# Stores of weight halves leave SP's DMA queue for ACT's and POOL's

## The chip, the cores and the metric

The kernel runs on one core of a Trainium2 chip. The metric is the device time of one execution in microseconds. Five engines run beside each other and meet through semaphores: PE (matrix products), DVE and POOL (elementwise work, POOL cannot read the matrix accumulators), ACT (activations, copies, casts) and SP, which here does nothing but start DMA transfers. Each engine, SP too, works its own list of instructions strictly in order: an instruction that waits holds up all that stand behind it on that engine. A DMA transfer is started by an instruction on some engine's list, and from there on runs by itself on the core's 16 DMA engines.

## The reference

One decoder layer on 2048 tokens of width 1024, in float32:

```
proj = x @ w_in                                  # 3592 columns, split over three mixers
y    = [GatedDeltaNet(4 heads) | dilated window attention(4) | differential attention(4)] @ w_out
x    = LayerNorm(alpha * x + y)
u    = causal depthwise conv3(x @ w_up)          # 2 x 2752 columns, gate and value
f    = (silu(gate) * value) @ w_down
out  = LayerNorm(alpha * x + f)
```

The gated delta rule is computed in chunks with a triangular inverse per chunk and a state carried from chunk to chunk. The window attention merges three dilations by their log-sum-exp; the differential attention subtracts two softmax maps.

## The kernel before

**Tiling.** Tokens come in four blocks of 512 (`NB = 4`, `TB = 512`). Channels lie on the 128 partitions. A product of a 128-column weight tile with a token block sums over eight slices of 128 (`KD = 8`) and fills one accumulator bank of 128x512.

**Three matmuls for one.** To keep float32 accuracy each operand is split into a rounded head and a rest: `hi` is the float32r cast, `lo` the difference. Each slice costs three matmuls, `whi*xhi`, `whi*xlo`, `wlo*xhi` (lines 206 to 208; for the output projections 1158, 1159, 1161).

**Weights** (`Dense.weights`, lines 127 to 162). A weight tile is handled as two halves of 128x512. The first time it is needed, each half is loaded by SP (`wraw`, line 151), ACT casts it to the head `whi` (line 153) and POOL subtracts to get the rest `wlo` (line 154). From job `c` of the plan on (`dn.keep = True`, line 1300) heads and rests of a tile with a key are also stored to DRAM, to `whi_d` and `wlo_d` (line 161), so that the later token blocks load them ready-made (line 148) and need neither ACT nor POOL. A head or rest may be overwritten only when its matmuls are done and its store has landed.

**Buffers.** Up to the end of the delta-rule phase raw halves, heads and rests have rings of 6, 4 and 4 buffers (`NRAW`, `NHALF`). Then all three kinds share one ring of 14 (`NW = 14`, line 1328). A half takes three of them, so a load can be at most between four and five halves ahead of the buffers it takes over.

**Stages.** The first phase does input projections and the first attention blocks (`FIRST`, line 1374). The second (`SECOND`) runs the delta rule: inverses, chunk preparation and the recurrence, with the projections of later blocks woven in; job `A3` there is the first whose weights are stored. The third (`THIRD`, line 1376) has the remaining attention blocks `w1 d1 A2 d2 w2 w3 d3` and the feed-forward blocks `f0` to `f3`, one per 512 tokens. Block `f0` meets every `w_up` and `w_down` tile for the first time, so it loads raw weights, splits and stores them; `f1` to `f3` load the stored halves. The part of `f2` that projects the mixers' output of the last token block (`attend(3)`) needs the attention block `d3` finished.

**What sets the order.** The code is written as jobs, but the place of each instruction on its engine is chosen when the program is built, by a scheduler that plays the program through a timeline of its own and takes what it holds to be ready. Attention work is mixed with feed-forward products in this way. Each DMA started from SP or ACT is also given one of eight shared completion counters, each started from POOL one of another eight; an instruction that starts a transfer on a counter waits until the counter's last transfer has landed, unless that is known already.

Some lines are named later: line 736 loads keys for the differential attention, lines 833 and 818 are its scores and its values on PE, line 835 its exponentials on ACT, line 700 stores its queries and keys, and line 595 scales the delta rule's output on POOL.

Of the kernel before, what the change touches and what calls it, by code (L numbers as in the profile page):

```python
# [27 lines left out]
def cast(x):  # L28
    return x.bitcast(F32)
# [81 lines left out]
class Dense:  # L111
# [15 lines left out]
    def weights(self, src, k=KD, m=P, pool=None, key=None):  # L127


        nc = self.nc  # L130
        n = k // 2 * m
        shape = lambda w: w.rearrange("p (k m) -> p k m", k=k // 2)

        def put(dt, name):
            if pool:
                w = pool.tile([P, TB], dt, tag=name, name=name, bufs=12)
            elif self.ring:
                w = self.wp.tile([P, TB], dt, tag="w", name=name, bufs=self.ring)
            else:
                w = self.wp.tile([P, TB], dt, tag=name, name=name, bufs=NRAW if name == "wraw" else NHALF)  # L140
            return shape(w[:, 0:n])

        his, los = [], []
        for i in range(2):
            if key in self.kept:
                hi, lo = put(F32R, "whi"), put(F32R, "wlo")
                for part, d in zip((hi, lo), self.kept[key]):
                    nc.sync.dma_start(out=cast(part), in_=cast(shape(d[:, i * n : i * n + n])))
            else:
                raw = shape((self.wp.tile([P, TB], F32, tag="w" if self.ring else "wraw", name="wraw", bufs=self.ring or NRAW))[:, 0:n])  # L150
                nc.sync.dma_start(out=raw, in_=src[:, i * (k // 2) : (i + 1) * (k // 2)])
                hi, lo = put(F32R, "whi"), put(F32R, "wlo")
                nc.scalar.copy(hi, raw)  # L153
                nc.gpsimd.tensor_tensor(out=lo, in0=raw, in1=hi, op=ALU.subtract)  # L154
            his.append(hi)
            los.append(lo)
        if key is not None and self.keep and key not in self.kept:
            self.kept[key] = [self.tc.dram_tile([P, 1024], F32R, name=name) for name in ("whi_d", "wlo_d")]
            for parts, d in zip((his, los), self.kept[key]):
                for i in range(2):  # L160
                    nc.sync.dma_start(out=cast(shape(d[:, i * n : i * n + n])), in_=cast(parts[i]))
        return Halves(his), Halves(los)

    def split(self, raw, pool=None, tag="x", bufs=None):
# [1290 lines left out]
```

## Time and profile before

| what | value |
|---|---|
| runs | 3291.5 us median of 3 (3281.3 to 3293.2) |
| profiled execution, its own time | 3290.28 us |
| span of that execution | 3288.5 us |
| PE busy | 3033.3 us, 92% of the span |
| DVE, ACT, POOL busy | 1870.7, 1354.4, 660.0 us |
| DMA moved | 659.29 MB, 200 GB/s over the span |
| stores of heads and of rests | 170 and 170, 256 KB each, the first at 745.5 us, the last at 1881.0 us |

The profile's page gives the busy time of each engine, the chain of work that ended last, and groups of instructions. Further views of the trace are used below: a table by stretch (busy time of each engine, number of instructions, granted PE clock, share of the DMA engines' time, GB/s), the chain of waits for a stretch, and lists of who waited for whom, for how many us in total, how many times, and the longest. A busy PE is not a PE at its peak: matmuls overlap, so a group's mean duration is longer than its share of the engine's time.

### The profile page before, as it was taken

Reading aid. Unit: us, or ns where it says so; the run is one execution under the profiler, and the core shown is the slowest. Engines: PE = TensorE matmul, PEld = TensorE weight load, DVE = VectorE, ACT = ScalarE, POOL = GpSimd, SP = SyncE. Lnnn points to the kernel's source line nnn. Section 1 sums busy time; section 2 is a strip of 40 time slices with the busy share of each in tenths; the row PEclk is TensorE's granted clock in tenths of the full one; section 3 lists DMA queues with packets and bytes.
Section 4 is the critical chain, followed back from the end, with each engine's and each line's share of the span. In section 5 each row is a group of like instructions: output and inputs, shape, how many; then the busy total and the mean of one; then the engine's idle time right before and its main releaser. Section 6 shows DMA issues by size and latency. Waiting matters only on the chain.

```text
span 3288.5 us, 43511 instructions
## 1 busy us (share of the span) xinstructions
PE 3033.3 (92%) x14476; PEld 2318.8 (71%) x14476; DVE 1870.7 (57%) x3392; ACT 1354.4 (41%) x3188; POOL 660.0 (20%) x571
## 2 busy tenths in 40 slices
PE   7898989998597798898899899999999999999998
PEld 5676867786476675565656677778866668888887
DVE  2562759665346245656746675557884444474446
ACT  3653553644144134645744332235653432122213
POOL 4563545442230012242212200000000000000001
PEclk9999989999688898998999999999999999999999
DMA  6546364546797776666677676666874545776554
GB/s 207 168 141 213 121 211 138 156 138 209 247 306 249 240 242 201 199 205 209 203 226 235 215 251 198 183 183 195 261 220 154 162 142 189 243 240 194 192 186 147
DMA packets 474209, 659.29 MB, mean 200 GB/s; under 512 B 75169, under 2 KB 201633, under 8 KB 473217
## 3 DMA queue, kind: packets, MB, share of 16 engines
q1 hardware_dynamic: 473984, 656.52, 63.2%
q8 instruction: 115, 1.88, 0.2%
q14 instruction: 110, 0.89, 0.1%
HBM read 500.82 MB, written 155.39 MB: 200 GB/s over the span
## 4 chain that ended last, share of the span: by engine, by line
PE 56%; DMA 12%; ACT 4%; DVE 3%; issue 2%; SPq 2%; POOL 1%; ACTq 0%; POOLq 0%; DVEq 0%
PE d L208 9%; PE d L206 9%; PE d L207 9%; PE rp L1158 6%; PE rp L1159 6%; PE rp L1161 5%; DMA wraw<-in_w_up 5%; PE bank L818 3%; DMA wraw<-in_w_down 3%; PE bank L833 2%; ACT whi L153 2%; PE bank L997 1%; DMA ks<-fk_d 1%; PE bank L1004 1%; PE bank L767 1%
## 5 line engine op out<-in xcount | busy, mean ns | idle before, releaser
L206 PE MATMUL d<-xhi,whi 128*128 128x512 f32 x2144 | 865.6, 404 | 41.1 <-ACT whi L153 16.4
L208 PE MATMUL d<-xhi,wlo 128*128 128x512 f32 x2144 | 861.3, 402 | 27.8 <-DMA wlo<-wlo_d 14.4
L207 PE MATMUL d<-xlo,whi 128*128 128x512 f32 x2144 | 858.9, 401 | 1.1 <-DVE xlo L169 1.1
L154 POOL TENSOR_TENSOR wlo<-wraw,whi 128x512 fp32r<-128x512 f32 x370 | 504.1, 1367 | 1471.1 <-ACT whi L153 1331.5
L206 PEld LDWEIGHTS d<-xhi,whi 128*128 128x128 f32 x2144 | 412.9, 193 | 153.0 <-ACT whi L153 26.2
L208 PEld LDWEIGHTS d<-xhi,wlo 128*128 128x128 f32 x2144 | 412.0, 192 | 136.8 <-POOL wlo L154 23.3
L207 PEld LDWEIGHTS d<-xlo,whi 128*128 128x128 f32 x2144 | 412.7, 192 | 102.8 <-issue 17.8
L153 ACT CAST whi<-wraw 128x512 fp32r<-128x512 f32 x370 | 227.7, 618 | 390.8 <-DMA wraw<-in_w_up 118.5
L1159 PE MATMUL rp<-wlo,hhi 128*128 128x512 f32 x704 | 280.9, 400 | 2.0 <-POOL wlo L154 2.0
L1158 PE MATMUL rp<-whi,hhi 128*128 128x512 f32 x704 | 268.1, 402 | 12.9 <-ACT whi L153 11.9
L1161 PE MATMUL rp<-whi,hlo 128*128 128x512 f32 x672 | 263.7, 396 | 0.0
L776 ACT ACTIVATE bank<-bank,nm 128x512 f32<-128x512 f32 (+3 forms) x320 | 190.1, 594 | 100.9 <-DVE nm L772 65.2
L1090 ACT COPY ub<-d 128x512 f32<-128x512 f32 x172 | 100.8, 586 | 315.9 <-PE d L208 315.3
L772 DVE TENSOR_REDUCE nm<-bank 128x1 f32<-128x512 f32 (+3 forms) x288 | 164.7, 598 | 96.1 <-PE bank L767 89.6
L843 POOL TENSOR_SCALAR_AFFINE_SELECT pd<-pd 128x128 f32<-128x128 f32 x64 | 32.5, 512 | 854.9 <-DVE pd L839 851.1
L839 DVE SCALAR_TENSOR_TENSOR pd<-pe,f_nlam,pd 128x512 f32<-128x512 f32 (+3 forms) x160 | 124.0, 782 | 138.3 <-ACT pe L835 109.6
L1158 PEld LDWEIGHTS rp<-whi,hhi 128*128 128x128 f32 x704 | 131.7, 189 | 55.4 <-ACT whi L153 19.1
L1159 PEld LDWEIGHTS rp<-wlo,hhi 128*128 128x128 f32 x704 | 133.5, 190 | 39.2 <-issue 6.9
L365 DVE SCALAR_TENSOR_TENSOR yc<-ub,i_taps,yc 128x512 f32<-128x512 f32 x144 | 156.3, 1086 | 3.3
L1168 DVE TENSOR_TENSOR r<-r,rp 128x512 f32<-128x512 f32 x152 | 101.8, 684 | 91.5 <-PE rp L1161 87.0
L1161 PEld LDWEIGHTS rp<-whi,hlo 128*128 128x128 f32 x672 | 127.3, 189 | 31.2 <-issue 4.8
L818 PE MATMUL bank<-pd,fv 128*64 128x512 f32 (+3 forms) x320 | 143.4, 553 | 0.0
(281 smaller groups left out, 4545.7 us busy)
## 6 DMA issues: line engine op xcount, KB each, us to landing
whi<-whi_d SPq DMA_DIRECT2D x486, 256.0 KB
wlo<-wlo_d SPq DMA_DIRECT2D x486, 256.0 KB
whi_d<-whi SPq DMA_DIRECT2D x170, 256.0 KB
wlo_d<-wlo SPq DMA_DIRECT2D x170, 256.0 KB
wraw<-in_w_gdn SPq DMA_DIRECT2D x128, 256.0 KB
ks<-fk_d SPq DMA_DIRECT2D x160, 196.0 KB
wraw<-in_w_up SPq DMA_DIRECT2D x86, 256.0 KB
wraw<-in_w_down SPq DMA_DIRECT2D x50, 256.0 KB
```

The costliest lines, as they stand in the source:

```text
L153: nc.scalar.copy(hi, raw)
L154: nc.gpsimd.tensor_tensor(out=lo, in0=raw, in1=hi, op=ALU.subtract)
L206: nc.tensor.matmul(out=ps, lhsT=whi[:, k], rhs=xhi[k], start=(k == 0), stop=False)
L207: nc.tensor.matmul(out=ps, lhsT=whi[:, k], rhs=xlo[k], start=False, stop=False)
L208: nc.tensor.matmul(out=ps, lhsT=wlo[:, k], rhs=xhi[k], start=False, stop=(k == KD - 1))
L365: nc.vector.scalar_tensor_tensor(out=yc, in0=ub[:, j : j + TB], scalar=self.taps[:, mt, j : j + 1], in1=yc, op0=ALU.mult, op1=ALU.add)
L772: nc.vector.tensor_reduce(out=o, in_=s[:, 0:nf], axis=mybir.AxisListType.X, op=ALU.min)
L776: nc.scalar.activation(out=s[:, 0:n], in_=s[:, 0:n], func=AF.Exp, scale=-1.0, bias=o, accum_out=den[:, b, m, qt : qt + 1])
L818: nc.tensor.matmul(out=po[64 * hh : 64 * hh + 64, q0:], lhsT=v[:, 64 * hh : 64 * hh + 64], rhs=pd[hh][:, q0:], start=start, stop=stop)
L1158: nc.tensor.matmul(out=ps, lhsT=hi[:, sl], rhs=whi, start=first, stop=False)
L1159: nc.tensor.matmul(out=ps, lhsT=hi[:, sl], rhs=wlo, start=False, stop=last and lo is None)
L1161: nc.tensor.matmul(out=ps, lhsT=lo[:, sl], rhs=whi, start=False, stop=last)
```

## The change

In `Dense.weights` the four stores of a tile are started from other engines: those of the heads from ACT, those of the rests from POOL. Nothing that is computed, loaded or stored differs; the transfers have the same sizes and addresses.

```
-            for parts, d in zip((his, los), self.kept[key]):
+            for eng, parts, d in zip((nc.scalar, nc.gpsimd), (his, los), self.kept[key]):
                 for i in range(2):
-                    nc.sync.dma_start(out=cast(shape(d[:, i * n : i * n + n])), in_=cast(parts[i]))
+                    eng.dma_start(out=cast(shape(d[:, i * n : i * n + n])), in_=cast(parts[i]))
```

The scheduler then lays the whole program out anew from there. Three places follow.

The first is SP's list in `f0`, while raw halves of `w_down` are loaded between the attention's keys (`ks`) and values (`fv`). Before:

```order
L736 DMA ks<-fk_d 98x4x128
L151 DMA wraw<-in_w_down 128x512
L161 DMA whi_d<-whi 128x512
L161 DMA wlo_d<-wlo 128x512
L161 DMA whi_d<-whi 128x512
L151 DMA wraw<-in_w_down 128x512
L826 DMA fv<-fv_d 128x128
L161 DMA wlo_d<-wlo 128x512
L161 DMA whi_d<-whi 128x512
L151 DMA wraw<-in_w_down 128x512
```

And with the change:

```order
L736 DMA ks<-fk_d 98x4x128
L151 DMA wraw<-in_w_down 128x512 x2
L826 DMA fv<-fv_d 128x128
L151 DMA wraw<-in_w_down 128x512
L736 DMA ks<-fk_d 98x4x128
L869 DMA y_d<-ob 128x512
L151 DMA wraw<-in_w_down 128x512 x2
```

Between one load of a raw half and the next there stood a store of a head and mostly one of a rest; now the loads follow each other, two in a row at places.

The second is ACT's list in `f0`, among the exponentials of the attention (line 776) and the copies of the convolution (lines 1090, 1091). Now there stands, where before only the casts stood:

```order
L153 CAST whi<-wraw 128x512
L161 DMA whi_d<-whi 128x512
L776 ACTIVATE bank_9714,den<-bank_9714,nm 128x256
L153 CAST whi<-wraw 128x512
L161 DMA whi_d<-whi 128x512
L776 ACTIVATE bank_9713,den<-bank_9713,nm 128x128
L776 ACTIVATE bank_9715,den<-bank_9715,nm 128x384
L776 ACTIVATE bank_9712,den<-bank_9712,nm 128x512
L153 CAST whi<-wraw 128x512
L161 DMA whi_d<-whi 128x512
L1090 COPY ub<-d 128x512
```

Each store stands right behind its cast or one or two instructions later. POOL's list alternates the subtraction and the store of its result in the same way.

The third is PE's list in `f2`, at the end of the attention block `d3`. Before, its last scores (line 833) and values (line 818) stood among products of `f2`:

```order
L208 MATMUL d<-xhi,wlo 128x512
L206 MATMUL d<-xhi,whi 128x512
L833 MATMUL bank_9712<-qs,ks 128x128
L207 MATMUL d<-xlo,whi 128x512
L208 MATMUL d<-xhi,wlo 128x512
L206 MATMUL d<-xhi,whi 128x512
L207 MATMUL d<-xlo,whi 128x512
L818 MATMUL bank_9715<-pd,fv 64x256
```

With the change the products end earlier, and the attention's last 96 matmuls (61 of line 833, 33 of line 818, 2 of line 865) stand in one piece, of which this is the beginning:

```order
L208 MATMUL d<-xhi,wlo 128x512
L833 MATMUL bank_9713<-qs,ks 128x512
L818 MATMUL bank_9715<-pd,fv 64x128
L833 MATMUL bank_9712<-qs,ks 128x512
L818 MATMUL bank_9715<-pd,fv 64x512
L833 MATMUL bank_9713<-qs,ks 128x512
L833 MATMUL bank_9712<-qs,ks 128x512
```

Part of the attention that stood inside `f0` now stands in `f1` and `f2`: PE's list from the first product of `f0` to the first of `f1` has 2149 matmuls instead of 2352.

## The prediction

> **What bounds the kernel now.** I read first the page's shares of the chain of waits, then the table by stretch from the first store to the end, then the chain inside the stretch that the first told me to look at, and last the lists of waits. On the page the chain lies on PE for 56% and on DMA for 12%, and the line under it names the raw loads of `w_up`, which are used in one stretch only:
>
> ```profile
> PE 56%; DMA 12%; ACT 4%; DVE 3%; issue 2%; SPq 2%; POOL 1%; ACTq 0%; POOLq 0%; DVEq 0%
> ```
>
> The table's columns are the stretch, its length, busy time and number of instructions of PE, weight loads, DVE, ACT and POOL, the granted PE clock, the DMA engines' share and GB/s:
>
> ```profile
> 745.00:1200.00 455.00, 351.36 (x2178) 286.06 (x2177) 197.81 (x441) 148.33 (x366) 79.15 (x69) 0.85 0.80 254
> 1200.00:1300.00 100.00, 87.13 (x426) 63.83 (x424) 59.64 (x108) 40.30 (x97) 27.02 (x21) 0.91 0.65 203
> 1300.00:1420.00 120.00, 107.39 (x403) 69.91 (x403) 77.18 (x180) 77.08 (x207) 36.42 (x32) 0.99 0.64 200
> 1420.00:1500.00 80.00, 77.36 (x296) 50.10 (x296) 41.92 (x52) 35.14 (x76) 31.91 (x30) 1.00 0.62 201
> 1500.00:1640.00 140.00, 119.83 (x429) 83.96 (x427) 94.57 (x206) 96.96 (x265) 38.16 (x28) 0.90 0.67 207
> 1640.00:1764.00 124.00, 122.10 (x448) 75.10 (x448) 58.36 (x91) 60.94 (x120) 23.25 (x25) 1.00 0.74 228
> 1764.00:1880.00 116.00, 106.52 (x445) 73.15 (x445) 81.45 (x119) 50.79 (x105) 37.00 (x32) 0.97 0.68 215
> 1880.00:3288.00 1408.00, 1395.96 (x6380) 1080.97 (x6379) 824.50 (x1450) 477.50 (x1100) 22.01 (x27) 1.00 0.62 197
> ```
>
> Behind 1880, where no half is stored any more, PE idles for 12 of 1408 us. In `f0`, 1200 to 1880, it idles for 680 - 620.3 = 59.7 us, nearly all of it in four rows (12.9, 12.6, 20.2, 9.5), and in three of these the clock is below 1. The delta-rule stretch before idles for 104 us, at a clock of 0.85. Inside `f0` the chain and one of its turns read (start, us, what):
>
> ```profile
> by line: DMA wraw<-in_w_up 21.8%; DMA wraw<-in_w_down 12.5%; ACT whi L153 6.6%; PE bank L818 5.6%; PE rp L1158 5.0%; issue 4.9%; PE rp L1159 4.3%; PE rp L1161 4.1%; PE bank L833 3.3%; DMA ks<-fk_d 2.8%; SPq L161 2.7%; PE d L208 2.6%; PE d L
> ```
>
> ```profile
> 1546.89 3.88 DMA wraw<-in_w_down
> ...
> 1550.85 0.63 ACT whi L153
> ...
> 1551.49 0.32 SPq L161
> ...
> 1551.86 4.97 DMA wraw<-in_w_down
> ```
>
> This is the bound. A load lands, ACT casts it, SP, which has been waiting for that cast in order to store it, starts the store, and only then the next load, which stands behind the store in SP's list. One half is in flight at a time, 4.97 us from load to load here, although the ring would hold four. SP's waits between 1300 and 1900 say the same (us in total, times, longest):
>
> ```profile
> SPq L161 <- ACT whi L153: 185.7, 78, 4.5
> SPq L161 <- POOL wlo L154: 37.6, 65, 1.1
> ```
>
> **The change part by part.** *The chain in `f0`.* The stores go from SP's list and with them the 223 us that SP waits in them. A load then waits for buffers alone. Three of 14 buffers go to a half, so load n takes over one whose user was four or five halves ahead: the subtraction of half n-4, or a head or rest whose matmuls and store are done. Four loads can be in flight, and a turn of load, cast and subtraction counts once for four halves. PE and the other engines set the pace. How much idle time stays is shown by the rows of `f0` where the chain did not decide: 1.9 of 124 us (1.5%) and 2.6 of 80 us (3.3%). On 620 us of PE work that is 9 to 20 us. I take 18, because bare runs of products in the new order use up halves faster than the mean. Gain 59.7 - 18 = 42 us; bounds 0 (another chain as long) and 50.
>
> *The clock.* Busy time times the missing share of clock is 87.13 x 0.09 + 107.39 x 0.01 + 119.83 x 0.10 + 106.52 x 0.03 = 24 us in `f0`. The rows with least idle time have 1.00, so shorter gaps should give some of it back: I take half, 12 us, bounds 0 and 24.
>
> *Two lists that become longer.* The prices come from these rows (count, then minimum, median and maximum in ns):
>
> ```profile
> L161 SPq DMA_DIRECT2D whi_d<-whi x170: 319/320/3069, 745.5 to 1879.6; - x170
> L153 ACT CAST whi<-wraw x128: 601/620/650, 1200.6 to 1878.9; 128x512 fp32r<-128x512 f32 x128
> L154 POOL TENSOR_TENSOR wlo<-wraw,whi x128: 1263/1286/2255, 1201.3 to 1879.6; 128x512 fp32r<-128x512 f32 x128
> ```
>
> ACT gets 128 stores in `f0`. No store stands on ACT yet; from below I bound it by SP's minimum of 0.319 us, from above by SP's 3.07. At the median, the nearest row, it is 41 us, beside 361 busy of 680 (the rows' sum), so it is hidden: ACT's spare time covers up to 2.5 us a store. Queued behind are casts, exponentials and copies of the convolution, each 0.32 us later. POOL gets as many, of which no row shows the like. Lower bound again 0.319. Upper bound is POOL's longest operation of this size, 2.26; I take 1.3, about its usual one. `f0` without the idle time, and without the attention that the new order takes out of it (203 matmuls at 620.3 us for the rows' 2447, about 50 us), lasts some 575 us, 4.5 a half, which leaves 3.2 us beside the subtraction. So both bounds are hidden and the cost is nothing; above 3.2 us POOL would be the new bound. The Trainium skill, "DMA: Bandwidth & Descriptors", section "Latency and other measured facts", gives about 1 us to the first byte for DMAs issued from GpSimd and 0.6 us for the hardware path; no run so far shows the former, and with it the sum stays the same.
>
> *The delta-rule stretch.* Of the 42 stores outside `f0` nearly all lie in 745 to 1200. PE's waits there that a quicker weight path could shorten, and the one that a fuller POOL could lengthen:
>
> ```profile
> PE vp L656 <- POOL wlo L154: 17.4, 6, 8.9
> PE yp L598 <- POOL on L595: 16.5, 4, 6.9
> PE vp L655 <- ACT whi L153: 8.8, 2, 7.0
> PE d L206 <- ACT whi L153: 6.6, 1, 6.6
> ```
>
> The first, third and fourth are 33 us, an upper bound of the gain. Against it, 42 x (0.32 + 1.3) = 68 us of new work lie on engines that the recurrence waits for; were a third of it on the path, 23 us would be lost. DMA is 80% busy there, so transfers begun earlier partly wait for each other instead. I take 0, bounds -23 and 33.
>
> *The end of `d3`.* The new order has 61 scores and 33 values in one piece in `f2`, with no product between them:
>
> ```profile
> L833 PE MATMUL bank<-qs,ks x128: 221/396/505, 2396.4 to 2693.4; 98*128 98x512 f32 x104, 98*128 98x384 f32 x8, 98*128 98x256 f32 x8, 98*128 98x128 f32 x8
> L818 PE MATMUL bank<-pd,fv x128: 272/592/643, 2423.6 to 2701.0; 128*64 128x512 f32 x104, 128*64 128x384 f32 x8, 128*64 128x256 f32 x8, 128*64 128x128 f32 x8
> L835 ACT ACTIVATE pe<-bank x64: 273/597/603, 2418.7 to 2693.6; 128x512 f32<-128x512 f32 x52, 128x384 f32<-128x384 f32 x4, 128x256 f32<-128x256 f32 x4, 128x128 f32<-128x128 f32 x4
> ```
>
> PE needs 61 x 0.396 + 33 x 0.592 = 44 us, ACT 61 x 0.597 = 36. With three banks in turn PE stays the longer, and the loss is 0; if each score waited for the exponential before it, it would be 36. I take 6.
>
> The sum: 42 + 12 + 0 - 6 = 48 us off the profiled execution's 3290.3 gives **3242 us**. That execution is 1.2 us below the median of the runs, so nothing is added.
>
> **The rivals.** *Only issue time is saved.* The loads wait again, for buffers whose stores are still on the way, and what goes is SP's own step in the chain: 2.7% of 680 = 18 us, 3272 us. For it: a buffer is released only by a landed store, and POOL's stores are unmeasured. Against it: the ring is four halves deep, and behind 1880 the same ring serves products at 1% idle. The Trainium skill, "DMA: Bandwidth & Descriptors", section "Issuing engines are not separate DMA queues", says that starting DMAs from several engines saves only the sequencer's time to start them, usually small; it is the rule that speaks against this change, and by it the sum would be this rival's 18 us. The trace speaks against it: what SP loses are 223 us of waiting, with 128 x 0.32 = 41 us of issue per kind of store.
>
> *Slower: ACT waits for SP's transfers.* In the delta-rule stretch 34 of the 40 head stores of the projections in `A3` and `o0` wait on a counter last used by a transfer of SP's. Such transfers take long there:
>
> ```profile
> 755.69 4.47 DMA whi_d<-whi
> 811.48 11.33 DMA qk<-qk_d
> 878.65 13.78 DMA fk_d<-sy
> ```
>
> If each of the 34 holds ACT for 4.5 us, the shortest of these, ACT loses 153 us in a stretch where it has 307 spare, and casts, exponentials and state copies of the recurrence stand behind. With half of it on the path the loss is 76 us and the time 3290 - 48 + 76 = 3318. It decides from 2.8 us a store. Against it: a counter comes round after eight transfers, so mostly the earlier one has landed.
>
> *The displaced attention.* The end of `d3` costs 36 us in place of 6: 3272 us. For it speaks the bare piece, which nothing covers; against it, that three banks take the scores in turn, so that PE need not wait for the exponential just before.
>
> **How the numbers follow.** Forecast 66%, only issue time 14%, displaced attention 7%, ACT's waits 13%. About 0.5%, 16 us, can be told from no change here, so faster means below 3275. The forecast lies there with all of its weight, the two cases at 3272 with half: 66 + 10 = 76% faster. The other half and a quarter of ACT's waits are the same: 14%. Slower: 10%. The forecast's own range is 3205 to 3270: at the low end all 24 us of clock and a quarter of the delta-rule bound come in, at the high end half of the gain in `f0` fails. With the rivals at 3272 inside and half of the slower case outside, the range is 3198 to 3288.
>
> **What would show it.** Right: in a table of the changed kernel, `f0` ends some 90 to 110 us earlier (48 and the moved attention), its chain no longer names raw loads, SP waits for PE in its loads, PE's idle time from 1200 on is near 30 us in all. Wrong: stores on POOL above 3 us; ACT waiting for DMA in line 161; the delta-rule stretch ending more than 20 us later; a gap on PE in the bare piece of `d3`.

## The result and the profile after

The changed kernel takes **3213.5 us** (median of 4 runs, 3209.9 to 3217.7), the kernel before on the same chip 3292.3 us (median of 4, 3281.3 to 3293.2). The ratio is 0.977, with a 95% interval from 0.976 to 0.979: 2.3% faster. The time lies inside the range and 28.5 us below the forecast of 3242. The profiled execution of the changed kernel took 3217.7 us, the one of before 3290.3, so the two traces differ by 72.6 us, and these are what has to be found in them.

The page of the changed kernel, first the two queues of its DMA transfers that are new (packets, MB, share of 16 engines), then the chain of work that ended last by engine:

```profile
q10 hardware_dynamic: 24480, 44.58, 3.8%
q0 software_dynamic: 13600, 44.58, 3.7%
...
PE 62%; DMA 7%; DVE 5%; ACT 2%; issue 1%; SPq 1%; POOL 1%; ACTq 0%; DVEq 0%; POOLq 0%
```

The stores have queues of their own, 44.58 MB each. DMA in the chain went from 12% to 7%, PE from 56% to 62%.

The table by stretch of the changed kernel (columns as in the prediction). `f0` is now 1184.6 to 1714.6, from its first cast to the last store; in the kernel before these two were 1200.6 and 1881.0:

```profile
745.00:1184.60 439.60, 341.98 (x2119) 275.97 (x2119) 191.27 (x426) 142.02 (x355) 96.03 (x106) 0.85 0.80 256
1184.60:1300.00 115.40, 113.62 (x589) 89.14 (x588) 84.75 (x148) 60.40 (x143) 63.59 (x65) 1.00 0.82 267
1300.00:1420.00 120.00, 118.86 (x489) 87.25 (x488) 84.33 (x175) 77.95 (x200) 65.00 (x71) 1.00 0.76 252
1420.00:1560.00 140.00, 134.99 (x535) 94.81 (x534) 82.76 (x105) 70.02 (x154) 75.95 (x87) 0.98 0.73 238
1560.00:1714.60 154.60, 143.78 (x616) 114.34 (x615) 123.47 (x223) 95.43 (x246) 54.28 (x56) 0.97 0.79 260
1714.60:2690.00 975.40, 970.43 (x4484) 718.32 (x4483) 598.77 (x1157) 392.29 (x915) 10.42 (x27) 1.00 0.62 196
2690.00:2740.00 50.00, 48.39 (x123) 15.28 (x121) 26.25 (x37) 35.16 (x67) 2.68 (x6) 1.00 0.28 82
```

In `f0` PE is busy for 511.3 of 530 us, so it idles for 18.7 where it idled for 59.7. The transfers run at 238 to 267 GB/s there, where the rows of before showed 200 to 228.

The 72.5 us of span split into three pieces. From the first cast of `f0` to the end, before 2087.9 us and now 2031.4, PE's idle time fell from 72.2 to 37.4 us: 34.8. Its busy time fell from 2015.7 to 1994.0: 21.7. And `f0` begins at 1184.6 and not at 1200.6: 16.0.

The last piece is not all waiting that went. Ahead of the first cast of `f0` PE now runs 5609 matmuls and not 5660, the others stand behind it, and it is busy there for 1005.8 us instead of 1017.6; its idle time there fell from 183.0 to 178.8. Over the whole span PE's idle time fell by 39.0 us, and its busy time, for the same 14476 matmuls, by 33.5.

What SP waits for in `f0`, and the chain there, in the changed kernel:

```profile
SPq L736 <- PE bank L767: 92.3, 24, 8.5
SPq L826 <- PE bank L818: 52.9, 11, 7.4
SPq L151 <- POOL wlo L154: 37.1, 19, 4.5
SPq L151 <- PE d L208: 36.2, 13, 3.7
```

```profile
by line: PE d L206 9.4%; PE d L208 9.4%; PE d L207 9.2%; PE rp L1158 8.2%; PE rp L1159 8.1%; PE rp L1161 7.9%; PE bank L818 5.1%; DVE nm L772 3.7%; PE bank L767 3.5%; DMA wraw<-in_w_up 3.5%; DVE yv L1095 2.8%; PE bank L833 2.5%; ACT bank L7
```

Line 161 is gone from SP's list. SP now waits for buffers, of keys and values (lines 736, 826) and of raw halves (line 151), most of them held by PE's own work. The chain is PE's products; of the raw loads, which carried 34% of it, those of `w_up` are at 3.5% and those of `w_down` below 1%.

The price of the stores on their new engines (count, then minimum, median and maximum in ns, first and last start), from the answers on `whi_d` and `wlo_d`:

```profile
L161 ACTq DMA_DIRECT2D whi_d<-whi x170: 326/326/614, 742.4 to 1712.9; - x170
```

```profile
L161 POOL DMA_DIRECT2D wlo_d<-wlo x170: 542/559/855, 746.0 to 1714.6; - x170
```

### The profile page after: what moved, and what is told of

Read it like the earlier page. It is cut to its first block, busy times and chain, and to the rows that moved or that the text cites. A ratio compares the mean times of both kernels' runs of the same rounds, so it can differ in the third digit from the quotient of the medians.

```text
span 3216.0 us, 43559 instructions
## 1 busy us (share of the span) xinstructions
PE 2999.8 (93%) x14476; PEld 2310.5 (72%) x14476; DVE 1883.0 (59%) x3392; ACT 1358.5 (42%) x3188; POOL 751.0 (23%) x741
## 3 DMA queue, kind: packets, MB, share of 16 engines
q10 hardware_dynamic: 24480, 44.58, 3.8%
q0 software_dynamic: 13600, 44.58, 3.7%
## 4 chain that ended last, share of the span: by engine, by line
PE 62%; DMA 7%; DVE 5%; ACT 2%; issue 1%; SPq 1%; POOL 1%; ACTq 0%; DVEq 0%; POOLq 0%
PE d L206 10%; PE d L207 10%; PE d L208 10%; PE rp L1158 6%; PE rp L1159 6%; PE rp L1161 6%; PE bank L818 4%; PE bank L833 2%; PE bank L767 1%; PE bank L997 1%; DMA whi<-whi_d 1%; PE bank L1004 1%; PE bank L958 1%; DMA fq_d<-sy 1%; DVE nm L772 1%
## 5 line engine op out<-in xcount | busy, mean ns | idle before, releaser
L839 DVE SCALAR_TENSOR_TENSOR pd<-pe,f_nlam,pd 128x512 f32<-128x512 f32 (+3 forms) x160 | 113.5, 715 | 168.1 <-ACT pe L835 142.6
```

## The experiments

All kernels compute and store everything. Each is laid out anew by the scheduler, so each carries an order of its own; the table at the end shows how far these orders differ. Ratios are to runs of the kernel before on the same chip, with 95% intervals. Diffs of the first six are against the kernel before, the others against the changed kernel.

### Heads alone

The stores of the heads go to ACT, those of the rests stay on SP.

```
-            for parts, d in zip((his, los), self.kept[key]):
+            for eng, parts, d in zip((nc.scalar, nc.sync), (his, los), self.kept[key]):
```

> Heads are stored from ACT, rests stay on SP. Theory 1 (what counts is which store stands ahead of the next load in SP's list): in f0 the store that is left there is that of the rest of the half before last, so two loads can be in flight; a turn of load, cast and subtraction, 4.0 + 0.6 + 1.3 us, counts for two halves, 3.0 us each, which is less than the 4.1 us a half that f0 took with the whole change. Most of the gain: 3215 to 3235 us. Theory 2 (SP saves issue time, so gain goes by the number of stores moved): half the gain, near 3253 us.

Measured: 3219.1 us, ratio 0.9795 (0.9765 to 0.9825): nearly the whole gain. What SP waits for in its `f0`:

```profile
SPq L161 <- POOL wlo L154: 225.9, 109, 4.8
```

SP waits for 226 us in the rests' stores (230 of 532 us in all rows of line 161, where it was 328 of 680 before), and the kernel loses next to nothing by it. Its list tells why. Here it is in time (start, us):

```profile
1405.04 0.38 SPq L826 DMA_DIRECT2D fv<-fv_d  x1
1405.47 0.45 SPq L151 DMA_DIRECT2D wraw<-in_w_up  x1
1407.68 0.32 SPq L161 DMA_DIRECT2D wlo_d<-wlo  x1
1408.06 0.42 SPq L151 DMA_DIRECT2D wraw<-in_w_up  x1
```

The store at 1407.68 comes 2.2 us after the load ahead of it. A load takes about 4 us (3.88 in the prediction's turn), the cast 0.62, the subtraction 1.29, so that store is of an earlier half, whose rest was still on its way when this load began. Two loads are in flight; from load to load it is 2.6 us in these rows, where the turn quoted of before took 4.97.

### Rests alone

The mirror image: rests on POOL, heads on SP.

```
+            for eng, parts, d in zip((nc.sync, nc.gpsimd), (his, los), self.kept[key]):
```

> Rests are stored from POOL, heads stay on SP. Theory 1: the store of a head still stands between its load and the next one, one half in flight, 4.0 + 0.6 + 0.3 us and more a half in f0: 3275 to 3295 us, and SP waits about as long for casts in line 161 as before (some 220 us). Theory 2: half the gain, near 3253 us.

Measured: 3292.6 us, ratio 1.0018 (1.0006 to 1.0030): no gain at all. What SP waits for in its `f0`, and a piece of its list:

```profile
SPq L161 <- ACT whi L153: 245.1, 92, 4.9
```

```profile
1513.93 0.33 SPq L151 DMA_DIRECT2D wraw<-in_w_up  x1
1517.87 0.32 SPq L161 DMA_DIRECT2D whi_d<-whi  x1
1518.29 0.37 SPq L151 DMA_DIRECT2D wraw<-in_w_up  x1
```

Load, 4 us, store of the head, next load: one half in flight, as before. The two runs take the same number of stores, 170, off SP's list, so the time that SP spends on starting them is the same in both; one gains 2% and the other nothing. The gain is not issue time. SP's waiting is not the loss either: in all rows of line 161 it waits for 230 us of the 532 of `f0` in the one and for 312 of 706 in the other, the same share. What costs is one store, standing between a load and the next, that needs that very load to have landed.

This is so for nearly all loads, not only in the rows shown. Counted from the starts in the traces, 123 of the 127 loads that start in `f0` of the kernel before start only when the cast of the half ahead of them has begun, and 127 of 129 with rests alone. With the change it is 33 of 128, with heads alone 44 of 128.

### The change in the feed-forward weights alone, and in the others alone

The first moves the stores of `w_up` and `w_down` only, which are those of `f0`, the second (with the two pairs exchanged) only those of the projections.

```
+            for eng, parts, d in zip((nc.scalar, nc.gpsimd) if key[0] in ("up", "down", "end") else (nc.sync, nc.sync), (his, los), self.kept[key]):
```

> The whole change for the weights of the feed-forward blocks alone (w_up, w_down): those of A3 and the output projection are stored from SP as before. From the two traces 56 of 73 us came behind the first cast of f0 and 16 before it. If these 16 belong to the stores of that stretch, this gives 3292 - 57 = 3235 us; if they are only another layout of the same waits, 3215 to 3250 us.

Measured: 3225.0 us, ratio 0.981 (0.978 to 0.984).

> The reverse: the change for the weights of A3 and the output projection alone, the feed-forward weights stored from SP. If the 16 us before f0 belong to these stores: 3276 us, with f0 as before (some 60 us of idle PE). If ACT or POOL lose there as much as SP gains: 3285 to 3300 us.

Measured: 3275.4 us, ratio 0.9963 (0.9950 to 0.9975). Medians against the 3288.5 of this chip's runs: 63 us and 13 us, together 76. So some 5/6 of the gain comes from the stores of `f0` (63 of 76). The rows of `f0` in the two kernels (first cast to last cast):

```profile
1189.10:1719.00 529.90, 511.23 (x2204) 385.04 (x2203) 370.23 (x639) 301.42 (x728) 262.90 (x276) 0.98 0.77 253
```

```profile
1181.60:1883.80 702.20, 645.23 (x2654) 434.10 (x2654) 428.28 (x812) 374.04 (x890) 192.37 (x165) 0.96 0.66 211
```

The first idles for 18.7 us in `f0`, like the whole change; the second for 57.0, like the kernel before. But `f0` begins 11.5 us earlier in the first too, although no store ahead of it changed its engine there, and 19.0 us in the second. With the new order PE has fewer matmuls ahead of `f0` in both, 5605 and 5609 instead of 5660. Its idle time there is 183.9 us in the first, where it was 183.0 before, and 173.1 in the second. So the earlier start of the first is work that now stands behind it, and only the second waits less.

### Both kinds on one engine

Both on POOL, then both on ACT (`nc.scalar` twice in the line below).

```
+            for eng, parts, d in zip((nc.gpsimd, nc.gpsimd), (his, los), self.kept[key]):
```

> Heads and rests are both stored from POOL, whose transfers have completion counters of their own; ACT starts none. A store took POOL 0.56 us in the trace of the change, so POOL has 1.29 + 2 x 0.56 = 2.4 us a half of 4.1. Theory that POOL has room and that ACT's waits on counters shared with SP cost little: 3205 to 3225 us. Theory that these waits (some 50 us of ACT before f0 with the whole change) cost on the path: 3190 to 3205 us.

Measured: 3230.5 us, ratio 0.9815 (0.9796 to 0.9833), above both ranges expected. A head's store on POOL:

```profile
L161 POOL DMA_DIRECT2D whi_d<-whi x170: 539/557/724, 747.2 to 1779.4; - x170
```

> Heads and rests are both stored from ACT. SP is as free as with the change, so theory 1 alone gives 3205 to 3225 us. But the store of a rest on ACT waits for POOL's subtraction, up to 1.3 us, with exponentials and copies behind it; 130 of these in f0 are up to 168 us of ACT, which has 226 spare there. If such waits on ACT reach the path: 3225 to 3270 us.

Measured: 3223.3 us, ratio 0.9789 (0.9771 to 0.9808). A rest's store on ACT:

```profile
L161 ACTq DMA_DIRECT2D wlo_d<-wlo x170: 326/326/898, 748.8 to 1719.7; - x170
```

Even 256 stores in `f0` are hidden, on ACT and nearly so on POOL. Which engine takes them matters little, as long as the heads' stores do not stand between the loads. The interval of the whole change (0.9756 to 0.9791) overlaps those of heads alone and of both on ACT, so POOL's share of the change can't be told from nothing; that of both on POOL lies just above it.

### A fuller POOL

The prediction said that up to 3.2 us a half would be hidden on POOL beside the subtraction. The changed kernel with the subtraction of each stored half made twice, then three times, with the same result:

```
-                nc.gpsimd.tensor_tensor(out=lo, in0=raw, in1=hi, op=ALU.subtract)
+                for _ in range(2 if key is not None and self.keep else 1):
+                    nc.gpsimd.tensor_tensor(out=lo, in0=raw, in1=hi, op=ALU.subtract)
```

> The changed kernel, with POOL's subtraction done twice for each half that is stored (same operands, same result): 2 x 1.29 + 0.56 = 3.1 us a half on POOL, below the 4.1 us that a half took in f0. If POOL's work is hidden up to about 3.2 us beside the subtraction, as the prediction reckoned, no change against the changed kernel: 3205 to 3225 us. If a store's price on POOL lies on the path, 170 x 1.29 = 219 us more POOL work would show by tens of us: 3240 us and more.

Measured: 3297.4 us, ratio 1.0024 (1.0006 to 1.0041). 1.35 us more a half, with the store 1.9 beside the first subtraction, and the whole gain is gone.

> The same with the subtraction done three times: 3 x 1.29 + 0.56 = 4.4 us a half on POOL, above the 4.1 us of a half in f0. POOL should now pace f0: 130 x 4.4 = 576 us instead of 529, and some of these 47 us show, as far as attention does not fill them: 3220 to 3262 us.

Measured: 3413.4 us, ratio 1.0372 (1.0353 to 1.0390), far above the 3220 to 3262 expected.

POOL itself was not full. With the doubled subtraction it still stood idle for 128 us of 500 (1200 to 1700) ahead of a subtraction, most of it for ACT's cast. The chain in that kernel's `f0` (line numbers are one higher) is led by VectorE, DVE in the rows:

```profile
by line: DVE yg L1096 6.0%; DVE yv L1096 5.8%; PE rp L1160 5.6%; PE rp L1159 5.3%; PE bank L819 5.3%; PE rp L1162 5.2%; DVE nm L773 4.8%; DVE pd L840 4.2%; issue 3.6%; DVE yv L1094 3.5%; DMA ks<-fk_d 3.4%; PE bank L834 3.1%; DVE hlo L1121 2
```

and its DVE instructions, the same ones on the same sizes, are longer. Groups of 1200 to 1700 us (count, busy us, mean ns), in the changed kernel:

```profile
L772 DVE TENSOR_REDUCE nm<-bank 128x1 f32<-128x512 f32 x95 | 61.8, 681 | 14.5 <-PE bank L767 10.9 <-DMA ks<-fk_d 3.5
L1095 DVE SCALAR_TENSOR_TENSOR yv<-ub,c_taps,yv 128x512 f32<-128x512 f32 x42 | 40.5, 964 | 0.9
L1093 DVE TENSOR_SCALAR yv<-ub,c_taps 128x512 f32<-128x512 f32 x21 | 15.9, 759 | 21.3 <-ACT ub L1090 21.2
L154 POOL TENSOR_TENSOR wlo<-wraw,whi 128x512 fp32r<-128x512 f32 x123 | 166.9, 1357 | 215.5 <-ACT whi L153 137.5 <-DMA yraw<-y_d 40.4 <-ACT c_halo L1091 14.0
```

and with the subtraction doubled:

```profile
L773 DVE TENSOR_REDUCE nm<-bank 128x1 f32<-128x512 f32 x96 | 61.6, 680 | 15.7 <-PE bank L768 13.9 <-DMA fv<-fv_d 1.8
L1096 DVE SCALAR_TENSOR_TENSOR yv<-ub,c_taps,yv 128x512 f32<-128x512 f32 x36 | 49.1, 1364 | 0.8
L1094 DVE TENSOR_SCALAR yv<-ub,c_taps 128x512 f32<-128x512 f32 x18 | 22.3, 1241 | 17.1 <-ACT ub L1091 17.1
L155 POOL TENSOR_TENSOR wlo<-wraw,whi 128x512 fp32r<-128x512 f32 x206 | 276.5, 1354 | 127.8 <-ACT whi L153 112.0 <-issue 8.7 <-PE bank L768 4.5
```

Behind `f0`, where POOL subtracts nothing, the two middle groups of the changed kernel take 749 and 484 ns. The maximum over an accumulator bank (`nm`), which reads nothing else, keeps its 0.68 to 0.69 us everywhere. The four experiments that follow ask whether it is POOL that holds VectorE up, and whether that is the loss.

### One more POOL operation of another kind

Ahead of the subtraction POOL copies the raw half into the rest's buffer; in the second kernel it fills the buffer with zeros. The subtraction then overwrites it.

```
+                if key is not None and self.keep:
+                    nc.gpsimd.tensor_copy(lo, raw)      # second kernel: nc.gpsimd.memset(cast(lo), 0.0)
                 nc.gpsimd.tensor_tensor(out=lo, in0=raw, in1=hi, op=ALU.subtract)
```

> The change whole, and ahead of the subtraction of each stored half POOL copies the raw half into the rest's buffer, which the subtraction then overwrites: one more POOL operation a half with one input in place of the two of the doubled subtraction. Theory 'POOL's reads of two inputs hold up VectorE': the taps of the convolution (line 1095, 0.93 to 0.96 us each in f0 with the change, 1.28 to 1.36 with the subtraction doubled) stay near 1.0 us, and the time is 3210 to 3240. Theory 'any element work on POOL holds up VectorE': taps at 1.2 us or more, 3260 to 3300. Theory 'POOL's own pace': if the copy takes as long as a subtraction, 1.35 us, the time is that of the doubled subtraction, 3290 to 3300, whatever the taps do.

Measured: 3278.4 us, ratio 0.9962 (0.9947 to 0.9976).

> The change whole, and ahead of the subtraction of each stored half POOL fills the rest's buffer with zeros, which the subtraction overwrites: one more POOL operation a half with no input. Theory 'POOL's reads hold up VectorE': taps of line 1095 as with the change, 0.93 to 0.98 us, and the time 3205 to 3230. Theory 'any element work on POOL': taps at 1.1 us or more and 3240 to 3300. Theory 'POOL's own pace': the time follows the length of the fill: 3215 to 3230 if it takes half a microsecond, 3290 if it takes as long as a subtraction.

Measured: 3225.6 us, ratio 0.9810 (0.9794 to 0.9825). The groups with the copy, then with the fill:

```profile
L1097 DVE SCALAR_TENSOR_TENSOR yv<-ub,c_taps,yv 128x512 f32<-128x512 f32 x36 | 33.2, 922 | 0.5
L155 POOL CAST wlo<-wraw 128x512 fp32r<-128x512 f32 x100 | 67.2, 672 | 209.0 <-DMA wraw<-in_w_up 62.7 <-PE d L209 37.3 <-PE bank L769 26.9
```

```profile
L1097 DVE SCALAR_TENSOR_TENSOR yv<-ub,c_taps,yv 128x512 f32<-128x512 f32 x42 | 41.0, 977 | 0.9
L155 POOL MEMSET wlo<- 128x512 f32 x122 | 65.8, 540 | 54.5 <-PE rp L1161 47.5 <-PE d L209 6.5
```

POOL's turn is 1.35 + 0.67 + 0.56 = 2.6 us with the copy and 1.36 + 0.54 + 0.56 = 2.5 with the fill, nearly the same; the times differ by 53 us. So POOL's own pace does not set the time. The taps are at 0.92 us with the copy, not longer than in the changed kernel, and still the kernel loses 65 us of the gain. So VectorE's longer instructions do not explain this loss either: no theory had it.

### The subtraction on VectorE

VectorE subtracts each stored half, in the second kernel every second one; POOL keeps the stores.

```
-                nc.gpsimd.tensor_tensor(out=lo, in0=raw, in1=hi, op=ALU.subtract)
+                (nc.vector if key is not None and self.keep else nc.gpsimd).tensor_tensor(out=lo, in0=raw, in1=hi, op=ALU.subtract)
```

> The change whole, but the subtraction of each stored half is made by VectorE (0.69 us for a subtraction of this size, line 1120 undisturbed) in place of POOL (1.35 us); POOL keeps the store of the rest. Theory 'POOL's subtraction holds up VectorE': in f0 the taps of line 1095 fall to 0.75 to 0.80 us, VectorE pays 128 x 0.69 = 88 us and gets some 45 us back of its 375 in a stretch of 529, so the time is 3195 to 3235. Rival 'what holds up VectorE in f0 is not POOL but the transfers': the taps stay at 0.93 us or more, VectorE has 463 of 529 us to do, and the time is 3235 to 3290.

Measured: 3229.4 us, ratio 0.9820 (0.9805 to 0.9834).

> As the run before, but only the second half of each weight is subtracted by VectorE, the first by POOL. Theory 'POOL's subtraction holds up VectorE': taps of line 1095 between 0.80 and 0.88 us, VectorE gains about half of what it pays, 3195 to 3225. Rival 'the transfers': taps at 0.93 us or more, 3215 to 3250.

Measured: 3220.4 us, ratio 0.9791 (0.9775 to 0.9807). The groups with all subtractions on VectorE, then with half of them:

```profile
L154 DVE TENSOR_TENSOR wlo<-wraw,whi 128x512 fp32r<-128x512 f32 x126 | 86.8, 690 | 43.6 <-ACT whi L153 42.0 <-DMA wlo_d<-wlo 1.5
L1095 DVE SCALAR_TENSOR_TENSOR yv<-ub,c_taps,yv 128x512 f32<-128x512 f32 x42 | 31.4, 747 | 0.5
L1093 DVE TENSOR_SCALAR yv<-ub,c_taps 128x512 f32<-128x512 f32 x21 | 10.2, 483 | 9.4 <-ACT ub L1090 9.1
```

```profile
L1095 DVE SCALAR_TENSOR_TENSOR yv<-ub,c_taps,yv 128x512 f32<-128x512 f32 x42 | 37.1, 884 | 0.9
```

With no subtraction on POOL the taps are back at 747 ns, while the DMA engines move as much as with the change (260 and 254 GB/s in `f0`). It is POOL's subtraction that holds VectorE up, and not the transfers. But lifting it gains nothing: neither kernel is faster than the changed one. In the first `f0` lasts 514.8 us in place of 530.0 and begins 16.9 us later.

### All runs beside each other

Worked out from the rows by stretch and the groups of each trace: `f0` (to the last store, in the two kernels that move one kind of weights to the last cast), PE's idle time in it, the part of it in which PE waits for a head or a rest (all its rows that name `whi` or `wlo`), the loads of raw halves that start only when the cast of the half ahead has begun, the matmuls of the two kinds of attention that the order has put into `f0`, and the mean of the taps `yv` between 1200 and 1700 us.

| kernel | us | ratio | `f0` from, to | PE idle in it | of it for a head or rest | loads behind the cast ahead | attention matmuls in it | taps, ns |
|---|---|---|---|---|---|---|---|---|
| before | 3292.3 | 1 | 1200.6, 1881.0 | 59.7 | 31.2 | 123 of 127 | 706 | 836 |
| the change | 3213.5 | 0.977 | 1184.6, 1714.6 | 18.7 | 0.6 | 33 of 128 | 463 | 964 |
| heads alone | 3219.1 | 0.980 | 1184.4, 1716.6 | 21.9 | 0.7 | 44 of 128 | 459 | |
| rests alone | 3292.6 | 1.002 | 1187.2, 1893.4 | 68.0 | 25.9 | 127 of 129 | 829 | |
| feed-forward alone | 3225.0 | 0.981 | 1189.1, 1719.0 | 18.7 | 0.4 | 30 of 128 | 461 | |
| projections alone | 3275.4 | 0.996 | 1181.6, 1883.8 | 57.0 | 28.2 | 127 of 129 | 894 | |
| both on POOL | 3230.5 | 0.982 | 1203.2, 1780.0 | 23.1 | 2.8 | 50 of 128 | 583 | |
| both on ACT | 3223.3 | 0.979 | 1190.8, 1719.7 | 18.7 | 1.0 | 22 of 128 | 473 | |
| subtraction twice | 3297.4 | 1.002 | 1195.5, 1864.1 | 66.9 | 13.5 | 38 of 128 | 650 | 1364 |
| three times | 3413.4 | 1.037 | 1225.4, 2093.3 | 137.0 | 23.7 | 74 of 128 | 1370 | 1325 |
| copy ahead | 3278.4 | 0.996 | 1188.7, 1888.4 | 71.8 | 6.9 | 58 of 129 | 862 | 922 |
| fill ahead | 3225.6 | 0.981 | 1188.2, 1721.1 | 22.8 | 0.0 | 37 of 127 | 456 | 977 |
| all on VectorE | 3229.4 | 0.982 | 1201.5, 1716.3 | 15.0 | 0.3 | 31 of 128 | 452 | 747 |
| half on VectorE | 3220.4 | 0.979 | 1188.0, 1706.8 | 16.7 | 0.2 | 29 of 128 | 453 | 884 |

The kernels fall into two groups. Those at 0.982 or less idle for 15 to 23 us in `f0`, whatever their taps take; those at 0.996 or more idle for 57 us or more, and have 650 or more attention matmuls in it. For rests alone and projections alone the reason is the store behind the load, still on SP: nearly every load starts behind the cast ahead of it, and PE waits for heads and rests for 26 and 28 us, as it did in the kernel before (PE's waits in `f0` there):

```profile
PE rp L1158 <- ACT whi L153: 11.9, 11, 1.9
PE d L206 <- ACT whi L153: 8.9, 12, 1.4
PE d L208 <- POOL wlo L154: 8.4, 18, 1.2
```

In the kernels of the first group these waits are nearly gone, 0 to 3 us. The copy and the repeated subtractions have no such store, and one load in flight is not the rule there. PE waits for heads and rests for 7 to 24 us, and for the larger part of its idle time ahead of the attention's own products: 64 of 72 us with the copy, 51 of 67 and 105 of 137 with the subtraction two and three times. With the copy:

```profile
PE bank L769 <- ACT bank L778: 19.8, 34, 2.6
PE bank L769 <- DMA ks<-fk_d: 17.6, 4, 11.1
```

So these three are as slow as the kernel before, or slower, for another reason in the main. Their order brings more attention into `f0`, with more keys and values on SP's list ahead of the raw halves; SP waits in those loads for 263 us with the copy (all rows of its lines 738 and 828), for 201 with the change and 104 with the fill. But with both kinds on POOL it waits for 256 us there, and that kernel loses little. Whether these three kernels lose by the order that the scheduler made for them, or by something that the added work on POOL does in any order, no run tells apart: it would need one order held fixed while POOL's work changes.

## Why the prediction was right

**The bound** was named rightly, and one thing more can be said of it now. The prediction's turn shows the head's store, but it counted 223 us of SP's waiting for both kinds of stores as what goes (all rows of line 161 in `f0` are 328 us). The runs with heads and with rests alone show that only the head's store carries the loss: it needs the load just ahead to have landed. The rest's store costs next to nothing where the order puts it behind a later load.

**The chain in `f0`: 42 us forecast, with 18 us left.** 18.7 us are left, so 59.7 - 18.7 = 41.0. This term was right nearly to the microsecond, and so was the way to it, the idle share of those rows in which the chain did not decide; the 18 itself was a choice between 9 and 20. Of the 41.0, 30.6 are PE's waits for heads and rests (31.2 to 0.6).

**The clock: 12 us forecast, half of 24.** Mis-sized. By the rows after, the missing clock in `f0` is 134.99 x 0.02 + 143.78 x 0.03 = 7.0 us, so 17 came back and not 12. (All four rows with idle time have a clock below 1, not three as the prediction says; its 24 us count all four.) PE's busy time over the span fell by 33.5 for the same matmuls; the remaining 16 us are in no row that I can name, and the forecast had no term for them.

**The stores on ACT and POOL: cost 0.** Right, with 0.33 us on ACT, close to SP's 0.32, and 0.56 on POOL, near the lower bound and not at the 1.3 us taken. The reason given with it was wrong in one place: "above 3.2 us POOL would be the new bound". With 1.9 us beside the subtraction, a doubled subtraction and the store, the kernel was already back at the time of before, in the order that it got, with POOL waiting for 128 us of the 500. POOL's free time in a stretch is not a price list for what can be put there.

**The delta-rule stretch: 0, bounds -23 to 33.** `f0` begins 16.0 us earlier, within the bounds, but only 4.2 of these are waiting that went (183.0 to 178.8 us of idle time ahead of it); the other 11.8 are busy time, with 51 matmuls fewer ahead of it. So for PE's waits the 0 was nearly right. With the feed-forward stores alone `f0` begins 11.5 earlier and with the projections' alone 19.0, with both on POOL 2.6 later, at 183.9, 173.1 and 199.0 us of idle time. Each of these is one order; what the stores alone do there stays open. PE's waits that were to give the gain (PE's waits from 740 us on, in the changed kernel):

```profile
PE vp L655 <- ACT whi L153: 17.7, 5, 5.5
PE d L206 <- DMA whi<-whi_d: 16.1, 2, 13.8
...
PE d L206 <- ACT whi L153: 7.4, 2, 5.3
```

The wait of line 656 for a rest, 17.4 us before, is down to 0.3; those for heads grew from 8.8 to 17.7 and from 6.6 to 7.4. Of the 33 us that bounded the gain, 33 - 25 = 8 went, and other waits took up part of that.

**The end of `d3`: -6.** Nearly nothing. PE's list in time there, in the changed kernel:

```profile
2710.97 0.73 PE L833 MATMUL bank<-qs,ks 98*128 98x512 f32 x2
2711.64 1.07 PE L818 MATMUL bank<-pd,fv 128*64 128x512 f32 x2
2712.64 0.73 PE L833 MATMUL bank<-qs,ks 98*128 98x512 f32 x2
```

Two scores and two values take 1.67 us (2710.97 to 2712.64), and of the 50 us from 2690 to 2740 PE idles for 1.6. The three banks hide the exponentials, as a loss of 0 would have it. But idle time behind `f0` did grow, from 12.5 to 18.6 us, spread over 1500 us with no wait above 2.3.

**The sum.** Forecast 42 + 12 + 0 - 6 = 48, measured 72.5. PE's idle time fell by 39.0 for 42 + 0 - 6 = 36. Nearly all of the 25 us that the forecast lacks is busy time, 33.5 for 12: the clock with 17, inside its bounds but taken too low, and 16 without a term. The range has more room than its own words give: a gain of 42 with all 24 us of clock, a quarter of the delta-rule bound (8) and the loss of 6 is 68 us, which ends at 3222 and not at 3205. The measured 3213.5 lies below that, so that the range holds it is in part luck.

**The signs foretold.** SP waits for PE in its loads, raw loads have nearly left the chain, idle time from `f0` on is 37 us for "near 30". `f0` ends 166 us earlier and not 90 to 110: the attention that the new order takes out of it is 243 matmuls (706 - 463) and not 203, and most of them are longer than the mean of all matmuls by which the 50 us were worked out: four scores and values in the bare piece take 1.67 us, 0.42 each, and the mean in `f0` was 620.7 us for 2444, 0.25 each. One sign of being wrong did appear, ACT waiting for DMA in line 161; it is answered next.

**The rivals.** "Only issue time" falls with heads alone and rests alone, which save the same issue time and differ by 2%. By the Trainium skill, "DMA: Bandwidth & Descriptors", section "Issuing engines are not separate DMA queues", starting transfers from several engines saves the sequencer's issue time only; the run with rests alone agrees (ratio 1.002), the one with heads alone does not (0.980), since there a wait goes with the store. "ACT waits for SP's transfers" came, but without its price. The longest store took 0.614 us and the list of waits shows none for ACT's queue, but ahead of the stores stand semaphore instructions of line 161, and between 776 and 976 us 15 of them ended a wait for a transfer, 14 times one of SP's with other data, as the rival had it: up to 7.7 us, about 50 in all. That is a third of the 153 us reckoned there, or 1.2 a store, below the 2.8 from which it would have decided; and PE's idle time ahead of `f0` did not grow. With both kinds on POOL, ACT starts no store and has no such waits, and the kernel is not faster (3230.5). "Displaced attention" did not come either, as the rows of `d3` show.

## What to carry to other kernels

On an engine that starts transfers in order, look for a store that waits for the result of the load just ahead of it: it allows one load in flight, however deep the ring. It is that store that must go to another list, or behind the next load; how long the engine waits in total tells nothing (230 of 532 us without the loss, 312 of 706 with all of it). Count instead how many loads start only when the half ahead has been cast. And where a program's order is made anew with every edit, compare idle time in the stretch, and what it is spent on, as well as total times: with the feed-forward stores alone `f0` began 11.5 us earlier, although no store ahead of it had changed its engine.

## What the runs showed of the hardware

A subtraction on POOL lengthens VectorE's instructions that read SBUF at the same time. POOL subtracted for 0, 85.9, 166.9 and 276.5 us of the 500 from 1200 to 1700; a tap with two tensor inputs took 747, 884, 964 and 1364 ns, and one with a single input 483, 575, 759 and 1241. A maximum over an accumulator bank stayed at 680 to 685. These are the taps of the convolution's values; those of its gates go the same way (747, 894, 930, 1277 and 482, 510, 706, 1186). The lengthening does not simply grow with POOL's time: the kernel before has 836 beside 136.9 us of subtraction, both on POOL 974 beside 147.8, and with the subtraction made three times (310.3 us) the values' taps took 1325 and 637, those of the gates 1481 and 1765. So more than POOL's time counts. A fill on POOL, which reads nothing, did next to nothing to the taps with two inputs (977 against 964, gates 948 against 930). Of those with a single input the values' stayed (753 against 759) and the gates' took 967 against 706; no run tells whether that is the fill or the order.

The Trainium skill, "SBUF — State Buffer", section "SBUF: two separate sides", tells that VectorE and GpSimd share one pair of ports, which one instruction holds alone until it ends; instructions of VectorE with two SBUF inputs meet it only against a GpSimd operation that reads SBUF. For the taps with two inputs the subtraction and the fill agree with that. For the copy, which reads too, it stays open: 922 ns beside 136.7 us of subtraction lies between the 836 and the 974 above.

A store started on POOL took 0.56 us of POOL, one on ACT 0.33 of ACT's queue.
